# Low key parts doubled per head, so that the second score and low-rank products contract 128 rows

## The chip, the core and the metric

The kernel runs on one core of a Trainium2 chip: TensorE multiplies matrices out of SBUF into PSUM, VectorE, ScalarE and GpSimd work element by element, and DMA queues bring data from HBM. The metric is the device time of one execution in microseconds (us), lower is better. Times come from runs on the chip and from one execution recorded by the hardware profiler.

## What is computed

Two blocks of a network on 512 tokens of width 1024, all in float32. The first block has a convolution, an mLSTM and a feed-forward part. The second has two layers: the first mixes tokens by attention in three branches (compressed, selected and windowed keys), the second by a recurrent mixer; both also attend to 256 memory rows, and both end in a feed-forward part. What matters here:

```python
# attention layer, per branch (12 heads of 64, 4 groups of keys)
s_w = jnp.einsum('bqgrd,bkgd->bgrqk', qc, kwc) * scale - slopes * dist_w
p_w = _masked_softmax(s_w, mask_w)
o_w = jnp.einsum('bgrqk,bkgd->bqgrd', p_w, vwc)
...
# memory attention, both layers (4 heads of 64, 256 rows)
s = jnp.einsum('bshd,bmhd->bhsm', q, k) * (HEAD_DIM ** -0.5)
...
# recurrent mixer: low-rank decay and learning rate (64 wide)
w_log = -jax.nn.softplus(-(w0 + jnp.tanh(zw) @ w2)) - 0.5
a = jax.nn.sigmoid(a0 + za @ a2)
```

With 512 tokens every block of keys is among the selected ones, so that the selected branch is causal attention too.

## The kernel before

**Precision.** TensorE multiplies the type fp32r in one pass. To keep float32's precision the kernel splits an operand into a high part (fp32r) and a low part (the rest), and adds up high x high, high x low and low x high. In the dense products (`dense`, `products`) these are three products of 128 rows and 512 columns for each of the eight feature tiles.

**Heads of 64.** A head has only 64 features, and the array contracts 128 rows. `_stack` (line 1496) makes a tile per head of the queries that holds the high part on the head's own 64 partitions and the low part on the other 64. `_stack_k` (line 1510) makes a tile per head of the keys that holds the high part twice, on both halves, and one more tile for both heads with the low parts, each on its head's own 64 partitions. A score is then two products: the head's query tile against the doubled high key, over 128 rows (high x high and low x high), and the high half of the query against the low key, over 64 rows (high x low). The stationary operand is the query tile, 128 queries wide, so each product is preceded by a load of weights. `_stack_k` is called for the selected and the windowed keys of both pairs of groups in the attention and for the memory's keys in each layer, six times in all.

**Who uses it.** `_nsa_unit` (line 1576) is one block of 128 queries of two heads in one branch: per head the two products into a PSUM bank, an operation of VectorE that adds the distances out of PSUM and takes the minimum, and an exponential on ScalarE; then the division, transposes and the products with the values, 64 wide. A unit has 128, 256, 384 or 512 keys; there are 48 units, so 96 pairs of products. `_mem_att` (line 1376) does the same for the memory with 256 keys: 16 pairs in each layer. `_rw_prep` (line 1793) has two low-rank products for each of six pairs of heads, 512 columns wide: the weights' high part (stationary) against the stacked `zwa` over 128 rows, and the weights' low part against the high half of `zwa` over 64 rows. The low-rank weights come from DRAM with their 64 rows twice, so that `_rw_lora` splits a tile that is already doubled. The gate's low-rank product in `_rw_pair` (line 2094) has three parts of 128 rows and one of 96.

**Order of issue.** The order is written by the program beforehand. Units, memory attention and pairs of heads are generators; `_Side` steps them beside the dense products. `_Clock` estimates when each engine will be done with what was issued; its cost of an fp32r product depends on the columns alone, but the columns that it counts towards TensorE's activity are weighted with the part of the array that the stationary operand fills. `tick` lets steps run beside a dense product only while that activity is high (`hot`), and `keep_warm` issues products of zeros into an unread bank when it is low. All tiles come from 74 slots (`_Slots`) in a ring; a generator starts only if as many slots are free as its `need` says, and `_rw_pair` waits for 12. PSUM has eight banks, taken in the same way. VectorE also writes the low part of every dense weight tile (`wl`), ScalarE the high part (`wh`), both three tiles ahead.

In the profile every instruction carries line 359, that of the recording helper; tiles out of slots are called s, PSUM banks b, the mixer's stacked tiles k.

Of the kernel before, what the change touches and what calls it, by code (L numbers as in the profile page):

```python
# [237 lines left out]
def _region(x):  # L238
    """The partitions and columns of a piece of a tile on chip, or None."""
    if getattr(x.tensor, "_space", None) is None or "DRAM" in str(x.tensor._space):  # L240
        return None
    (w, n), rest = x.ap[0], x.ap[1:]
    p, f = divmod(x.offset, w) if w else (0, 0)
    return p, p + n, f, f + 1 + sum(abs(a) * (b - 1) for a, b in rest)


class _Clock:
    """When each engine comes to the end of what has been issued to it, as far as that is known beforehand: the order of
    issue follows from it."""
# [10 lines left out]
    def hot(self, least):  # L260
        """Whether the tensor engine's last window had so many columns: its clock halves when it idles."""
        while self.win and self.win[0][0] < self.t["tensor"] - WINDOW:
            self.cols -= self.win.popleft()[1]
        return self.cols >= least
# [82 lines left out]
class _Timed:  # L347
    """An engine, or the core, with every issue noted by the clock."""
# [43 lines left out]
def _run(g):  # L392
    """A generator's value, run to its end."""
    while True:
        try:
            next(g)
        except StopIteration as e:
            return e.value


class _Side:
    """Generators whose steps run beside the dense products: of the first few, those whose operands should be done by now."""
# [4 lines left out]
    def add(self, g, need=0, prio=0):  # L407
        """need: the slots that the generator will take, free before it starts; prio: the first of those ready."""
        B = self.B
        self.q.append([max(B.pe, B.clock.step) + B.lat, g, need, False, prio])  # L410
# [4 lines left out]
    def step(self, wait=True):  # L415
        """One step of the generator that is ready first; without wait, only if one is."""
        if not self.q:
            return False
        B = self.B
        n = self.free()  # L420
        e = min([e for e in self.q[:self.width] if e[3] or e[2] <= n] or self.q[:1],
                key=lambda e: (max(e[0], B.pe), -e[4], e[0]))
        if e[0] > B.pe:
            if not wait:
                return False
            B.keep_warm(e[0])
        step, B.clock.step = B.clock.step, 0.0
        e[3] = True
        t = B.sl.taken
        try:  # L430
            next(e[1])
            e[0] = max(B.pe, B.clock.step) + B.lat if B.clock.step else max(B.pe, e[0]) + POLL
            e[2] = max(0, e[2] - B.sl.taken + t)
        except StopIteration:
            self.q.remove(e)
        B.clock.step = max(step, B.clock.step)
        return True
# [6 lines left out]
class _B:  # L444
# [69 lines left out]
    def warm(self, on=True):  # L514
        """Whether zeros keep the tensor engine's clock up."""
        if on:
            z = self.sl.get()
            self.nc.gpsimd.memset(z, 0.0)
            self.zero, self.zps = self.sl.get(F32R), self.ps.get()
            self.acopy(self.zero, z)  # L520
            self.sl.put(z)
        else:
            self.sl.put(self.zero)
            self.ps.put(self.zps)
            self.zps = None

    def keep_warm(self, until):
        """Products of zeros into a bank that nobody reads."""
        while self.zps is not None and (self.pe + 300 < until or not (until or self.clock.hot(HOTF))):
            self.nc.tensor.matmul(self.zps, self.zero[:, 0:128], self.zero, start=True, stop=True)  # L530
# [57 lines left out]
    def hl_g(self, src, scale=None):  # L588
        """The high and the low part of src, or of src times a column: a generator."""
# [15 lines left out]
    def park(self, j):  # L605
        """x's tile to DRAM; its slot is free again."""
        self.nc.gpsimd.dma_start(self.xd[:, j, :], self.x[j])
        self.sl.put(self.x[j])
# [11 lines left out]
    def col_sums(self, accs, nb):  # L620
        """Sums over the partitions, per token: [128 tokens, nb] of each."""
        ps = self.ps.get()
        for i, acc in enumerate(accs):
            for b in range(nb):
                o = 2 * (nb * i + b)
                self.mm(ps[:, o:o + 2], acc[:, 128 * b:128 * b + 128], self.ones[:, 0:2])
        return ps

    def spread(self, cols, nb):
        """Columns [128 tokens, nb] -> the tokens' values on all partitions, in PSUM."""  # L630
# [8 lines left out]
    def rstd_g(self, acc, nb=4, in_psum=False):  # L639
        """Per token (mean of the squares + eps)^-0.5, on all partitions: a generator."""  # L640
# [17 lines left out]
    def rstd2(self, a1, a2):  # L658
        """r1 = rstd of a1's squares; r2 = r1 times the rstd of a2's squares scaled by r1."""
# [128 lines left out]
def _ada_dot(B, e, ts, cb):  # L788
    """One feature tile of the modulation: the rows of its weights times silu(c)."""
# [7 lines left out]
def _ada_side(B, cols, last=False):  # L797
    """Feature tiles of the modulation: a generator."""
# [10 lines left out]
def _mem_prep(B, out):  # L809
    """The memory's rows, split, times both layers' norm weights; their factors: a generator."""  # L810
# [54 lines left out]
def _start(B):  # L865
    """Block 1's h by feature tiles, as the modulation's weights come, and the first projections beside it, all of them open."""
# [46 lines left out]
    h = []  # L913
# [37 lines left out]
def _conv_ops(B, pairs, done):  # L951
    """The 31 taps of two channel tiles, their chains taken in turn, in PSUM."""
# [28 lines left out]
def _gates(B, ps):  # L981
    """Input and forget gates -> rows of the running maximum, columns of g and of exp(-m): a generator."""
# [32 lines left out]
def _mlstm(B, h, q, k, va):  # L1015
    """One head's stabilised memory read, normalised and scaled: a generator of steps."""
# [69 lines left out]
def _conv_ln(B):  # L1086
    """Layer norm over the channels and silu: a generator; leaves B.a."""
# [25 lines left out]
def _qk_conv(B, z, y, c, h):  # L1113
    """The causal convolution of four taps, the last already in y, and silu: a generator."""
# [216 lines left out]
def _ffn(B, h, u, d, sq, gcol, post, mid=None):  # L1331
    """x += g * (silu(h Wg) * (h Wu)) Wd; with sq, h still wants the tokens' factors, from the squares' sums sq."""
# [43 lines left out]
def _mem_att(B, i, t, q, cross):  # L1376
    """Attention of a q tile (two heads, scaled by -1/8) to the memory: a generator."""
# [8 lines left out]
    for hf in range(2):  # L1386
        r0, r1 = 64 * hf, 64 * hf + 64
        sm = B.mp.tile([128, 8], F32, tag="ms", name="ms", bufs=4)
        pr = []
        for bp in range(2):  # L1390
            ps = B.ps.get()
            for b in range(2):
# [3 lines left out]
                B.mm(o, q[hf][r0:r1, qb:qb + 128], B.memS[i][2][r0:r1, m], False, True)  # L1396
# [42 lines left out]
def _compress(B, st):  # L1439
    """Keys and values of the compressed blocks: a generator."""  # L1440
# [55 lines left out]
def _stack(B, z, out=None):  # L1496
    """Two heads' tile, split: per head [high; low], the high parts on the head's own partitions. A generator."""
# [12 lines left out]
def _stack_k(B, z, st, key):  # L1510
    """Two heads' keys, split: per head [high; high], and the low parts. A generator."""
# [6 lines left out]
    low = B.sl.get(F32R)  # L1518
    for hf, t in enumerate(out):
        a, b = slice(64 * hf, 64 * hf + 64), slice(64 - 64 * hf, 128 - 64 * hf)  # L1520
        B.tt(low[a], z[a], t[a].bitcast(F32), OP.subtract)
        B.vcopy(t[b], t[a])
    B.sl.put(z)
    st[key] = out + [low]


def _nsa_comp(B, i, q, st, P):
    """The compressed blocks' branch of two heads, which begins their sum: a generator."""
# [47 lines left out]
def _nsa_unit(B, i, br, b, st, P, mix):  # L1576
    """One block of queries of two heads in the selected or the windowed branch: a generator."""
# [11 lines left out]
    for hf in range(2):  # L1589
        r = 64 * hf  # L1590
# [3 lines left out]
        B.mm(ps[:, :n], q[r:r + 64], k[2][r:r + 64, 0:n], False, True)  # L1594
# [39 lines left out]
def _tok_major(B, src, st, key):  # L1634
    """A tile's transpose: a generator."""
# [26 lines left out]
def _nsa(B, xg, factors):  # L1662
# [8 lines left out]
    for n in NSA_ORDER:  # L1671
# [22 lines left out]
        else:  # L1694
# [5 lines left out]
            elif nm in ("ks", "kw"):  # L1700
                B.side.add(_stack_k(B, t, st, (nm, e)), 3)
# [14 lines left out]
def _wo(B, name, parts, g2):  # L1716
    """x += rhs Wo, in parts as the mixers' shares come; x * g2 in parts, the squares' sums."""
# [62 lines left out]
def _rw_lora(B, p, g):  # L1780
    """One pair's share of the low-rank weights, split: the high and the low parts, side by side. A generator."""
# [11 lines left out]
def _rw_prep(B, p, rkv, R):  # L1793
    """One pair of heads: decays, keys and their products, with the exponents taken about each chunk's middle: a generator."""
# [10 lines left out]
    B.mm(ps, lo[0:64, 256:384], R["zwa"][0][0:64], False, True)  # L1805
# [4 lines left out]
    B.mm(ps, lo[64:128, 384:512], R["zwa"][1][64:128], False, True)  # L1810
# [79 lines left out]
def _rw_blocks(t):  # L1890
    """The diagonal 16 x 16 blocks of [64, 64] matrices that lie 4160 apart: [block, row, column]."""
# [3 lines left out]
def _rw_rows(t):  # L1895
    """The same matrices: [row, matrix, column]."""
# [3 lines left out]
def _rw_inv(B, p, lt, R):  # L1900
    """The inverses of the diagonal 16 x 16 blocks of one pair's triangular matrices, by substitution: a generator."""
# [34 lines left out]
def _rw_half(B, out, ps, mask):  # L1936
    """Four blocks of 128 columns from PSUM, the latter half of each masked."""
# [5 lines left out]
def _rw_pair(B, p, rkv, R, mix):  # L1943
    """One pair of heads, from the projections to its share of the mix: a generator.

    A chunk and head gets the factors of [values | state], [tokens | keys, next state | outputs], whatever the state is.
    """
# [290 lines left out]
```

## Time and profile before

| | us |
|---|---|
| median of 3 runs | 2523.57 |
| lowest and highest run | 2523.26, 2525.66 |
| span of the profiled execution | 2516.8 |
| TensorE busy in the span | 2441.9 |
| VectorE busy | 1470.4 |
| ScalarE busy | 921.5 |
| GpSimd busy | 408.4 |

The span runs from the first to the last instruction. A busy share is an average over stages; the first block takes 540 us, the feed-forward parts some 400 each, the attention layer lies at 945 to 1320 us, the recurrent mixer at 1700 to 2060 us with its last products up to 2120. TensorE's busy time includes the way of a product through the array, so that two products in a row overlap in it; the distance between the starts of two weight loads (PEld) tells better what a product costs.

### The profile page before, as it was taken

The page shows a single profiled execution, that of the slowest core. Times are in us where ns is not written, and L with a number is a line of the kernel's source. Part 1 is how long each engine was busy: PE and PEld are TensorE (multiplying, and loading weights), DVE is VectorE, ACT ScalarE, POOL GpSimd, SP SyncE. Part 2 cuts the span into 40 slices and gives each one's busy share as a digit, 9 for nine tenths or more (in the row PEclk, how much of TensorE's full clock was granted, in tenths as well). Part 3 has the DMA queues.
Part 4 walks back from the last instruction along what each step waited for, and adds up shares of the span by engine and source line. Part 5 has one row for each costly group of instructions (what it writes and reads, how often), then busy time and mean ns, then how long its engine had stood idle before and what let it go on. Part 6 is the DMA issues. An engine that isn't in the chain of part 4 may idle for free.

```text
span 2516.8 us, 32883 instructions
## 1 busy us (share of the span) xinstructions
PE 2441.9 (97%) x12817; PEld 1951.5 (78%) x12817; DVE 1470.4 (58%) x2673; ACT 921.5 (37%) x1554; POOL 408.4 (16%) x523
## 2 busy tenths in 40 slices
PE   7999999899999999999999999999999999999997
PEld 5877778788888888766677888887777777888886
DVE  7998884867333345476775434446764646443443
ACT  5264445253322233345443222233443323222221
POOL 4433334200000012000002000021451432000000
PEclk8999999999999999989899999999999999999998
DMA  8221223725333234212113232243432231223222
GB/s 275 85 75 59 76 67 132 286 93 184 99 86 109 93 95 163 67 36 78 55 34 114 86 104 98 85 138 122 144 86 57 80 72 34 92 80 113 93 88 79
DMA packets 124956, 252.58 MB, mean 100 GB/s; under 512 B 48253, under 2 KB 54829, under 8 KB 124801
## 3 DMA queue, kind: packets, MB, share of 16 engines
q1 hardware_dynamic: 76096, 211.64, 26.2%
q0 software_dynamic: 10352, 32.74, 3.8%
q10 hardware_dynamic: 38352, 6.10, 1.4%
q8 instruction: 100, 1.64, 0.3%
q14 instruction: 56, 0.45, 0.1%
HBM read 234.69 MB, written 15.75 MB: 100 GB/s over the span
## 4 chain that ended last, share of the span: by engine, by line
PE 62%; issue 20%; DVE 12%; POOL 3%; ACT 2%; DMA 1%; POOLq 0%; SPq 0%; DVEq 0%; ACTq 0%
PE b L359 62%; DVE s L359 7%; DVE b L359 3%; POOL s L359 2%; ACT s L359 2%; DVE modc L359 1%; DVE wl L359 1%; ACT wh L359 0%; POOL gt L359 0%; DMA s<-in_w_ada_dram 0%; DMA s<-in_xT_dram 0%; DMA s<-in_w_in_dram 0%; DMA s<-ltd 0%; ACT L359 0%; DMA ident<-in_ident_dram 0%
## 5 line engine op out<-in xcount | busy, mean ns | idle before, releaser
L359 PE MATMUL b<-s,wh 128*128 128x512 f32 (+1 forms) x5456 | 1699.3, 393 | 6.8 <-DVE s L359 6.3
L359 PEld LDWEIGHTS b<-s,wh 128*128 128x128 f32 x5456 | 1018.2, 190 | 226.4 <-issue 10.6
L359 PE MATMUL b<-s,wl 128*128 128x512 f32 (+1 forms) x2728 | 1062.4, 389 | 8.2 <-DVE wl L359 8.2
L359 PEld LDWEIGHTS b<-s,wl 128*128 128x128 f32 x2728 | 516.6, 189 | 115.4 <-DVE wl L359 8.6
L359 DVE TENSOR_TENSOR wl<-wr,wh 128x1024 fp32r<-128x1024 f32 (+2 forms) x313 | 361.0, 1155 | 217.8 <-ACT wh L359 216.3
L359 ACT ACTIVATE wh<-wr 128x1024 fp32r<-128x1024 f32 (+2 forms) x371 | 364.2, 982 | 222.5 <-PE b L359 176.5
L359 DVE TENSOR_TENSOR s<-b,s 128x512 f32<-128x512 f32 (+4 forms) x338 | 200.9, 601 | 394.8 <-PE b L359 359.8
L359 ACT ACTIVATE s<-s 128x512 f32<-128x512 f32 (+5 forms) x315 | 189.0, 610 | 574.2 <-DVE s L359 558.2
L359 PE MATMUL b<-s,s 64*64 64x64 f32 (+13 forms) x2960 | 334.4, 290 | 14.2 <-DVE s L359 10.3
L359 PEld LDWEIGHTS b<-s,s 64*64 64x64 f32 (+3 forms) x2960 | 228.9, 150 | 122.9 <-issue 63.5
L359 DVE TENSOR_TENSOR s<-s,s 128x512 f32<-128x512 f32 (+5 forms) x308 | 196.0, 649 | 130.3 <-ACT s L359 128.3
L359 POOL TENSOR_TENSOR s<-s,s 128x512 f32<-128x512 f32 (+9 forms) x232 | 134.4, 583 | 566.8 <-ACT s L359 524.6
L359 ACT ACTIVATE s<-b 128x256 f32<-128x256 f32 (+5 forms) x257 | 110.7, 460 | 302.6 <-PE b L359 230.3
L359 POOL TENSOR_TENSOR wl<-wr,wh 128x1024 fp32r<-128x1024 f32 x58 | 143.0, 2466 | 254.3 <-ACT wh L359 245.0
L359 DVE SCALAR_TENSOR_TENSOR b<-s,par,b 128x511 f32<-128x511 f32 (+14 forms) x240 | 158.1, 731 | 0.0
L359 DVE SCALAR_TENSOR_TENSOR s<-s,par,s 128x511 f32<-128x511 f32 (+4 forms) x115 | 106.7, 938 | 30.9 <-ACT s L359 29.8
L359 PE MATMUL b<-s 128*128 128x512 f32 (+2 forms) x601 | 103.1, 338 | 0.0
L359 PE MATMUL b<-ident,s 128*128 128x128 f32 (+1 forms) x544 | 80.5, 281 | 13.7 <-DVE s L359 8.9
L359 PEld LDWEIGHTS b<-ident,s 128*128 128x128 f32 (+1 forms) x544 | 63.7, 143 | 32.5 <-DVE s L359 11.8
L359 POOL TENSOR_TENSOR rs_t<-rs_t,mhalf 128x4 f32<-128x4 f32 (+1 forms) x8 | 7.8, 981 | 467.2 <-DVE rs_t L359 467.2
L359 PEld LDWEIGHTS b<-s 128*128 128x128 f32 (+2 forms) x601 | 65.7, 174 | 17.2 <-issue 7.7
L359 ACT ACTIVATE s<-s,par 128x512 f32<-128x512 f32 (+2 forms) x72 | 48.2, 680 | 64.7 <-DVE s L359 64.2
(160 smaller groups left out, 1091.6 us busy)
## 6 DMA issues: line engine op xcount, KB each, us to landing
wr<-in_w_in_dram SPq DMA_DIRECT2D x59, 512.0 KB, 3.3
s<-in_w_ada_dram SPq DMA_DIRECT2D x96, 256.0 KB, 5.9
wr<-in_fu_dram SPq DMA_DIRECT2D x44, 512.0 KB, 3.3
wr<-in_f0u_dram SPq DMA_DIRECT2D x44, 512.0 KB, 3.3
wr<-in_f1u_dram SPq DMA_DIRECT2D x44, 512.0 KB, 3.3
wr<-in_w_rw_dram SPq DMA_DIRECT2D x23, 512.0 KB, 3.6
wr<-in_w_nsa_dram SPq DMA_DIRECT2D x21, 512.0 KB, 3.3
wr<-in_w_o_dram SPq DMA_DIRECT2D x16, 512.0 KB, 3.4
```

The lines of the kernel that those rows point to most:

```text
L359: r = f(*a, **k)
```

## The change

`_stack_k` makes two tiles of low parts instead of one, each with its head's low part on both halves of the partitions: two more copies on VectorE per call. The second product of a score then takes the whole query tile and the head's doubled low tile, over 128 rows; it now also adds low x low. The second low-rank products take all 128 rows of weights and of `zwa`, which were there already. The generators of the keys want 4 slots instead of 3. Docstrings and comments are taken out as well; nothing of them runs.

```diff
@@ _mem_att
-                B.mm(o, q[hf][r0:r1, qb:qb + 128], B.memS[i][2][r0:r1, m], False, True)
+                B.mm(o, q[hf][:, qb:qb + 128], B.memS[i][2 + hf][:, m], False, True)
@@ _stack_k
-    low = B.sl.get(F32R)
-    for hf, t in enumerate(out):
+    low = [B.sl.get(F32R), B.sl.get(F32R)]
+    for hf, (t, l) in enumerate(zip(out, low)):
         a, b = slice(64 * hf, 64 * hf + 64), slice(64 - 64 * hf, 128 - 64 * hf)
-        B.tt(low[a], z[a], t[a].bitcast(F32), OP.subtract)
+        B.tt(l[a], z[a], t[a].bitcast(F32), OP.subtract)
         B.vcopy(t[b], t[a])
+        B.vcopy(l[b], l[a])
     B.sl.put(z)
-    st[key] = out + [low]
+    st[key] = out + low
@@ _nsa_unit
-        B.mm(ps[:, :n], q[r:r + 64], k[2][r:r + 64, 0:n], False, True)
+        B.mm(ps[:, :n], q, k[2 + hf][:, 0:n], False, True)
@@ _nsa
-                B.side.add(_stack_k(B, t, st, (nm, e)), 3)
+                B.side.add(_stack_k(B, t, st, (nm, e)), 4)
@@ _rw_prep
-    B.mm(ps, lo[0:64, 256:384], R["zwa"][0][0:64], False, True)
+    B.mm(ps, lo[:, 256:384], R["zwa"][0], False, True)
...
-    B.mm(ps, lo[64:128, 384:512], R["zwa"][1][64:128], False, True)
+    B.mm(ps, lo[:, 384:512], R["zwa"][1], False, True)
```

## Rows read from the trace of the kernel before

**Rows 1.** The chain that ended last: its shares of the span by engine.

```profile
PE 62%; issue 20%; DVE 12%; POOL 3%; ACT 2%; DMA 1%; POOLq 0%; SPq 0%; DVEq 0%; ACTq 0%
```

**Rows 2.** Stretches: length, busy us (instructions) of PE, PEld, DVE, ACT, POOL, clock, DMA.

```profile
1045.00:1320.00 275.00, 271.03 (x1477) 189.77 (x1476) 197.64 (x571) 132.17 (x332) 12.58 (x21) 0.92 0.15 49
1700.00:2060.00 360.00, 353.72 (x2894) 270.27 (x2894) 216.76 (x505) 135.78 (x294) 133.42 (x292) 0.99 0.34 96
```

**Rows 3.** Who waited for whom, 1045 to 1320: us, times, longest.

```profile
PEld b L359 <- issue: 44.3, 170, 3.3
...
PE b L359 <- DVE s L359: 3.8, 3, 2.9
```

**Rows 4.** Timeline of weight loads, dense: start, length, [idle before].

```profile
1079.77 0.19 PEld L359 LDWEIGHTS b<-s,wl 128*128 128x128 f32 x1
1079.99 0.41 PEld L359 LDWEIGHTS b<-s,wh 128*128 128x128 f32 x2
1080.45 0.19 PEld L359 LDWEIGHTS b<-s,wl 128*128 128x128 f32 x1
```

**Rows 5.** Timeline of weight loads in units of 512 and of 384 keys.

```profile
1086.73 0.19 PEld L359 LDWEIGHTS b<-s,s 128*128 128x128 f32 x1 [0.25 <-issue]
1087.16 0.18 PEld L359 LDWEIGHTS b<-s,s 64*128 64x128 f32 x1 [0.25 <-issue]
1087.59 0.19 PEld L359 LDWEIGHTS b<-s,s 128*128 128x128 f32 x1 [0.24 <-DVE sm L359]
...
1103.33 0.18 PEld L359 LDWEIGHTS b<-s,s 64*128 64x128 f32 x1 [0.19 <-issue]
1103.70 0.19 PEld L359 LDWEIGHTS b<-s,s 128*128 128x128 f32 x1 [0.19 <-issue]
```

**Rows 6.** The same for 256 and then 128 keys, both shapes merged.

```profile
1172.45 1.12 PEld L359 LDWEIGHTS b<-s,s 128*128 128x128 f32 x4 [0.17 <-issue]
1173.70 0.95 PEld L359 LDWEIGHTS b<-s,s 128*128 128x128 f32 x4
```

**Rows 7.** Timeline of weight loads, dense products of 256 columns, three per row pair.

```profile
562.15 0.19 PEld L359 LDWEIGHTS b<-s,wl 128*128 128x128 f32 x1
...
562.51 0.19 PEld L359 LDWEIGHTS b<-s,wl 128*128 128x128 f32 x1
```

**Rows 8.** The gate's product: its 96-row form, and its loads.

```profile
L359 PE MATMUL b<-k,s 96*128 96x512 f32 x6 | 2.4, 399 | 0.0
...
1943.80 0.76 PEld L359 LDWEIGHTS b<-k,s 128*128 128x128 f32 x4
1944.93 1.07 PEld L359 LDWEIGHTS b<-s,s 64*64 64x64 f32 x36 [0.37 <-issue]
```

**Rows 9.** Products of 64 rows by form: 1045 to 1320, then 1700 to 2060.

```profile
L359 PE MATMUL b<-s,s 64*128 64x256 f32 x40 | 16.8, 420 | 0.0
L359 PE MATMUL b<-s,s 64*128 64x512 f32 x24 | 12.0, 499 | 0.0
L359 PE MATMUL b<-s,s 64*128 64x384 f32 x24 | 10.7, 445 | 0.0
L359 PE MATMUL b<-s,s 64*128 64x128 f32 x24 | 9.1, 379 | 0.0
...
L359 PE MATMUL b<-s,s 64*128 64x256 f32 x16 | 6.1, 381 | 0.0
L359 PE MATMUL b<-k,s 64*128 64x512 f32 x12 | 5.9, 495 | 0.0
```

**Rows 10.** Stretches with a burst of units, and one after it.

```profile
1085.80:1094.60 8.80, 8.80 (x22) 4.53 (x20) 5.66 (x19) 6.06 (x17) 0.00 (x0) 0.77 0.18 61
1110.30:1118.20 7.90, 4.78 (x36) 3.57 (x34) 7.66 (x19) 6.88 (x13) 0.00 (x0) 0.98 0.10 19
...
1242.00:1251.00 9.00, 9.00 (x25) 4.65 (x22) 6.09 (x20) 6.17 (x18) 0.00 (x0) 0.81 0.21 68
```

**Rows 11.** VectorE by form: count, busy us, mean ns; the second row is `_stack_k`'s copy.

```profile
L359 DVE CUSTOM_DVE_ANT_0 s<-b,s 128x512 f32<-128x512 f32 x24 | 16.6, 691 | 9.4 <-PE b L359 9.4
L359 DVE CAST s<-s 64x512 fp32r<-64x512 f32 x12 | 5.1, 424 | 0.2
```

More of the change, by code (lines that the diff above doesn't have):

```diff
@@ L1386, in _mem_att @@
     for hf in range(2):
-        r0, r1 = 64 * hf, 64 * hf + 64
         sm = B.mp.tile([128, 8], F32, tag="ms", name="ms", bufs=4)
@@ L1589, in _nsa_unit @@
     for hf in range(2):
-        r = 64 * hf
         ps = B.ps.get()
```

## The prediction

> **What bounds the kernel now.** I read the chain of work that ended last first: TensorE holds 62% of it and another 20% is "issue", time in which an engine waits for nothing that the profile shows [rows 1]. So the next question is where TensorE itself stands without a cause. The table by stretches gives the two places that the change touches: the attention of the second block (1045 to 1320 us) and the recurrent mixer (1700 to 2060 us). In both TensorE is busy nearly throughout (271.0 of 275 us, 353.7 of 360 us), VectorE 72% and 60%, and the granted clock is 0.92 in the first and 0.99 in the second [rows 2]. The waits in the attention say the same: TensorE's sequencer waited for VectorE for 3.8 us, but the weight loads sat idle before "issue" 170 times for 44.3 us [rows 3]. That idle time is what I look at, because nobody releases it.
>
> The order of weight loads shows where it lies. In the dense products three loads follow each other every 0.68 us (1079.77 to 1080.45), 0.227 us for a product of 512 columns, with no idle time noted: the load hides behind the product ahead of it [rows 4]. In a block of queries the loads of a 128-row and a 64-row product take turns, and each step takes 0.43 us at 512 columns and 0.37 us at 384, with 0.19 to 0.25 us of idle before every load [rows 5]. Four loads at 256 columns take 1.25 us from 1172.45 to 1173.70, so 0.313 us each; the four at 128 columns after them take (0.95 - 0.18) / 3, some 0.255 us each [rows 6]. Dense products of 256 columns step at 0.36 / 3 = 0.12 us [rows 7]. The 128-row and the 64-row product wait alike, so it isn't the size of the 64-row product that costs: it is the turn from one shape to the other. The strongest sign is the gate's low-rank product: its fourth part contracts 96 rows after three of 128, and the four loads lie together in 0.76 us without an idle time ahead of them; the next load, of 64 rows, again stood idle for 0.37 us [rows 8]. Ninety-six rows go with 128, 64 rows don't.
>
> **The change part by part.** (1) The second product of each score and of each low-rank pair gets 128 rows. There are 140: in the attention 24 each of 512, 384 and 128 columns and 40 of 256 (24 of the units, 16 of the memory), in the recurrent mixer 12 of 512 and 16 of 256 [rows 9]. The number of columns stays, so a product itself should cost what its dense neighbour costs. Each of them now pays for two turns, one into 64 rows and one out. What one turn costs, from the rows above: at 512 columns 0.43 - 0.227 = 0.203 us; at 384 0.37 - 0.173 = 0.197 us, where 0.173 is an estimate halfway between the dense steps at 256 and 512; at 256 0.313 - 0.12 = 0.193 us; at 128 0.255 - 0.12 = 0.135 us, where 0.12 is taken from the 256 columns as the nearest row and so is rather too much. Two turns for each: attention 24 x 0.406 + 24 x 0.394 + 40 x 0.386 + 24 x 0.27 = 9.7 + 9.5 + 15.4 + 6.5 = 41.1 us; mixer 12 x 0.406 + 16 x 0.386 = 4.9 + 6.2 = 11.1 us; together 52.2 us. The turn out stays where the next product is 64 wide anyway (values after scores): I estimate one in ten, 14 x 0.2 = 2.8 us off, 2 of it in the attention.
>
> (2) What is late next. In the attention the units come in bursts: ten heads' scores one after the other, ten pairs of products. The stretch from 1085.8 to 1094.6 us is one; five of them stand in the trace, that of 1242 is another [rows 10]. By the steps above its 20 products need 8 x 0.227 + 4 x 0.173 + 8 x 0.12 = 3.5 us without turns and 7.2 us with them at full clock. VectorE has 5.7 us of work in it [rows 10], because every head's score is read out of PSUM by an operation of 0.69 us at 512 columns [rows 11], and the eight banks let TensorE run ahead of it by a few heads only. I therefore let such a burst end after 5.5 us (between 3.5, if the banks hold it all, and 7.2, if TensorE waits for each head): 1.7 us saved of 3.7, 2 us given back in each, 10 us in five. In the stretch from 1110.3 to 1118.2 us VectorE is already the one that is waited for: it is busy for 7.7 of 7.9 us and TensorE for 4.8 [rows 10]; what is won shortly ahead of it, one set of six second products or 2 us, is lost there.
>
> (3) Twelve copies more on VectorE (two in each of six calls of `_stack_k`) at 0.424 us, the copy that is there already [rows 11]: 5.1 us, eight of them in the attention. Nearly all have cover, since VectorE has 77 us free there [rows 2]; the four of the second half of the keys can meet the stretch after 1110 us, where there is none. Bounds 0 and 5.1 us, I take 2. The low-rank part needs nothing new, its weights already stand twice in their tile.
>
> (4) The clock. 0.92 over 275 us means that 16% of it, 44 us, ran at 1.2 GHz instead of 2.4; the bursts show it, at 0.77 and 0.81 [rows 2, 10]. Work that would take 22 us took 44. After the change the same columns come in less time, and with full rows. Bounds: nothing, if the waits for VectorE take the place of the turns, and 22 us if all of it goes. The bursts' share is some two thirds, 15 us; I take half of that, 7.5.
>
> (5) The order of issue. The planner counts a product's columns by the part of the array that it fills, so each of the 140 now counts twice as much. That lets side steps start earlier and asks for fewer products of zeros; and the keys hold one slot of 74 more per tile (four, and one for the memory), with 4 free slots wanted instead of 3. No row prices this; it can go either way. In the mixer, where zeros are issued, it is 12 x 256 + 16 x 128 = 5120 columns more, ten products of zeros or 2.3 us at the most [rows 4]; I set it to nothing.
>
> (6) The mixer's 11.1 us: the low-rank products lie among dense work and should give their 4.9; the memory's 6.2 fall where TensorE also runs products of zeros while chains of other engines go on, and I take half. 8 us.
>
> The sum: attention 41.1 - 2 - 10 - 2 - 2 = 25.1; clock 7.5; mixer 8; together 40.6 us. The profiled span is 2516.8 us and the median of the runs 2523.57, so 6.8 us lie around the span; the change doesn't touch them. 2523.57 - 40.6 gives **2483 us**.
>
> One rule speaks against this. The Trainium skill, "TensorE: Matmul & The Clock Gate", section "Part 3: Packing small matmuls — row/col tiling", says that a weight load overlaps products in flight only where its row group is another one. By that rule two 128-row products in a row would not hide the second load, and the sum of (1) would be nothing. The trace disagrees: dense products, all of 128 rows, step at 0.227 us with loads of 0.19 us in between [rows 4].
>
> **The rivals.** A: all of it comes. The banks carry the bursts, the clock stays up and the planner asks for a few zeros less: 52.2 - 2.8 + 15 + 2 = 66 us, 2457 us. For it: VectorE is free for 77 us of the attention. Against it: it isn't free in the bursts.
>
> B: VectorE becomes the bound of the attention. Its 197.6 us and 3.4 of copies would then be 88% of a stretch of 230 us, and its steps come in chains. If the units' second phase waits as the bursts do, half of the attention's 25 us is lost, no clock comes back, and 12.5 + 8 = 20.5 us remain: 2503 us. For it: the stretch at 1110 us [rows 10]. Against it: VectorE waits far more for TensorE than the other way round.
>
> C: nothing comes, since the load of the second product can't hide behind a first one of the same row group. Mechanism here: load, product, load, product at 0.19 + 0.23 us, about the 0.43 of today [rows 4, 5]. Only the copies are left, 2525 us. The dense rows speak against it. It is what the rule of the Trainium skill named above would do.
>
> D, slower: the slots. Five slots fewer and a higher want per step hold the attention's units back until the dense products that cover them are used up. TensorE then stands as between 1110.3 and 1118.2 us, idle for 3.1 of 7.9 us, or 40% [rows 10]. One cycle of a query tile takes some 40 us, so each held cycle costs 16 us; three of the six cost 48, which is more than the gain: 2483 + 48 = 2531 us. It decides from the third cycle on. Against it: the attention isn't short of cover now, TensorE idles for 4 us of 275 [rows 2].
>
> **How the numbers follow.** Forecast 0.60, A 0.17, B 0.14, C 0.03, D 0.06. The forecast's own bounds come from (2), (4) and (5): bursts 7.2 or 3.5 us, clock 0 or 15, so 2468 to 2500. The range takes in A and B: 2455 to 2506 us, and leaves out C, D and the outer edge of the forecast. About 0.2% (5 us) is what a measurement of this kernel can tell from no change. Faster by more than that: forecast, A and B, 0.91. Within: C, 0.03. Slower: D, 0.06.
>
> **What would show it.** Right: the second products in the profile have 128 rows, the waits of weight loads before "issue" fall from 170 times in the attention to a third, pairs at 512 columns outside bursts step at 0.23 us, and the attention's stretch is about 33 us shorter, the mixer 8. In the bursts, idle time of TensorE ended by VectorE takes the place of "issue". The granted clock rises above 0.92. Wrong: pairs at 128 rows that still step at 0.43 us (C); TensorE waiting for VectorE for tens of us (B); loads of the next heads' tables that move by tens of us (D).

## The result, and the profile after

The changed kernel takes 2482.57 us (median of 4 runs, 2478.97 to 2483.98) against 2524.61 of the kernel before in the same comparison; the ratio is 0.9837, interval 0.9824 to 0.9851. The forecast was 2483 with 2455 to 2506. The whole came out as forecast; its parts didn't, and that is what the rest is about.

The two layers can be cut at the sums over the tokens' squares, four small products with a tile of ones that stand at the head of each layer's factors. In the traces they start at 955.9, 1333.1, 1698.0, 2140.7 us before and at 956.0, 1288.5, 1653.8, 2100.9 after. Between the first two lies the attention layer with its output product, between the last two the mixer with its own. The table by stretches of the kernel before for the two layers (length, busy us and instructions of TensorE, weight loads, VectorE, ScalarE, GpSimd, then the granted clock and the DMA):

```profile
956.00:1333.10 377.10, 368.62 (x1918) 268.51 (x1916) 250.27 (x649) 167.98 (x382) 40.01 (x68) 0.94 0.21 70
1698.00:2140.70 442.70, 432.18 (x3585) 330.51 (x3583) 266.00 (x615) 164.81 (x350) 149.35 (x304) 0.99 0.30 84
```

and of the changed kernel:

```profile
956.00:1288.50 332.50, 317.88 (x1918) 250.19 (x1916) 245.69 (x659) 162.18 (x382) 40.30 (x68) 0.98 0.24 80
1653.80:2100.90 447.10, 435.26 (x3629) 335.10 (x3627) 265.64 (x617) 162.33 (x350) 145.36 (x304) 1.00 0.29 84
```

The attention is 44.7 us shorter with the same number of products. The mixer is 4.4 us **longer**, with 45 products more, all of them of zeros (44 between the rounded edges of the rows). The span falls by 39.6 us, 2516.8 to 2477.2; the stretches outside the two layers differ by 0.4 us or less each.

The second products have 128 rows now, so that both products of a score stand in one row, twice the count of [rows 9] (products by form in the attention), and the copies of `_stack_k` have doubled (VectorE, whole trace; compare [rows 11]):

```profile
L359 PE MATMUL b<-s,s 128*128 128x256 f32 x80 | 14.1, 297 | 3.5 <-DVE s L359 3.5
L359 PE MATMUL b<-s,s 128*128 128x512 f32 x48 | 12.9, 406 | 0.0
L359 PE MATMUL b<-s,s 128*128 128x384 f32 x48 | 11.6, 357 | 3.5 <-DVE s L359 3.2 <-ACT s L359 0.4
L359 PE MATMUL b<-s,s 128*128 128x128 f32 x48 | 8.9, 291 | 0.5
...
L359 DVE CAST s<-s 64x512 fp32r<-64x512 f32 x24 | 9.3, 427 | 0.4
```

The waits of the attention after (who waited for whom, us, times, longest; 1045 to 1275 us), which answer to [rows 3]:

```profile
PEld b L359 <- issue: 23.1, 75, 3.1
PEld b L359 <- DVE s L359: 9.2, 10, 1.9
PE b L359 <- DVE s L359: 8.6, 7, 2.7
```

Of 170 waits without a releaser 75 are left, where a third was forecast, and 44.3 us became 23.1; TensorE's wait for VectorE has grown from 3.8 to 8.6 us. A burst of ten heads shows the gain at its purest. This is one in the timeline of weight loads, with its stretch behind it; compare the loads of [rows 5] and the stretch 1085.8 to 1094.6 of [rows 10]:

```profile
1079.34 3.09 PEld L359 LDWEIGHTS b<-s,s 128*128 128x128 f32 x16 [0.81 <-issue]
1082.70 0.30 PEld L359 LDWEIGHTS b<-s,s 128*128 128x128 f32 x2 [0.27 <-DVE sm L359]
1083.17 0.30 PEld L359 LDWEIGHTS b<-s,s 128*128 128x128 f32 x2 [0.18 <-DVE sm L359]
1083.39 0.30 PEld L359 LDWEIGHTS b<-s,wh 128*128 128x128 f32 x2
...
1078.40:1084.00 5.60, 5.50 (x28) 3.91 (x28) 5.12 (x16) 3.29 (x10) 0.00 (x0) 1.00 0.25 94
```

Sixteen loads in a row without an idle time ahead of any, then two short waits for VectorE: 20 products in 4.05 us (1079.34 to 1083.39) where the same burst took 8.7, and at full clock. The other four bursts took 4.05 to 4.31 us, where they took 7.3 to 8.4 before. VectorE is busy for 5.1 of 5.6 us.

What is late next is seen behind the bursts. In the timeline of all engines from 1218.5 us TensorE has loaded one head's scores and then stands idle for 1.9 us, while VectorE works off a weight tile's low part, a reciprocal, a small product, two scalings and two copies out of PSUM, of which the first ends the wait:

```profile
1218.10 1.22 DVE L359 TENSOR_TENSOR wl<-wr,wh 128x1024 fp32r<-128x1024 f32 x1
1218.55 0.30 PEld L359 LDWEIGHTS b<-s,s 128*128 128x128 f32 x2 [0.17 <-issue]
...
1219.62 0.48 DVE L359 TENSOR_SCALAR s<-s,sm 128x128 f32<-128x128 f32 x2
1220.02 1.15 DVE L359 COPY s<-b 128x512 f32<-128x512 f32 x2
1220.76 0.30 PEld L359 LDWEIGHTS b<-s,s 128*128 128x128 f32 x2 [1.91 <-DVE s L359]
```

### The profile page after: what moved, and what is told of

The parts are those of the page before. It is cut to its first block, busy times and chain, and to the rows that moved or that the text cites. A ratio compares the mean times of both kernels' runs of the same rounds, so it can differ in the third digit from the quotient of the medians.

```text
span 2477.2 us, 32995 instructions
## 1 busy us (share of the span) xinstructions
PE 2393.6 (97%) x12862; PEld 1937.2 (78%) x12862; DVE 1465.2 (59%) x2685; ACT 913.0 (37%) x1554; POOL 404.9 (16%) x523
## 4 chain that ended last, share of the span: by engine, by line
PE 62%; issue 17%; DVE 15%; ACT 2%; POOL 2%; DMA 1%; ACTq 0%; POOLq 0%; SPq 0%; DVEq 0%
PE b L359 62%; DVE s L359 9%; DVE b L359 3%; ACT s L359 2%; POOL s L359 1%; DVE wl L359 1%; DVE modc L359 1%; ACT wh L359 0%; POOL gt L359 0%; DMA s<-in_w_ada_dram 0%; DMA s<-ltd 0%; DVE st L359 0%; DMA s<-in_xT_dram 0%; DVE sm L359 0%; ACT L359 0%
## 5 line engine op out<-in xcount | busy, mean ns | idle before, releaser
L359 PE MATMUL b<-s,s 64*64 64x64 f32 (+9 forms) x2960 | 291.4, 280 | 18.8 <-DVE s L359 13.2
L359 PEld LDWEIGHTS b<-s,s 64*64 64x64 f32 (+3 forms) x2960 | 216.2, 149 | 99.0 <-issue 43.3
L359 POOL TENSOR_TENSOR s<-s,s 128x512 f32<-128x512 f32 (+9 forms) x232 | 128.5, 557 | 546.1 <-ACT s L359 499.2
L359 PE MATMUL b<-s 128*128 128x512 f32 (+2 forms) x646 | 118.4, 342 | 0.0
L359 PEld LDWEIGHTS b<-ident,s 128*128 128x128 f32 (+1 forms) x544 | 63.4, 142 | 35.0 <-DVE s L359 14.2
L359 PEld LDWEIGHTS b<-s 128*128 128x128 f32 (+2 forms) x646 | 71.7, 173 | 18.5 <-issue 5.3
```

The source lines that it names most:

```text
L359: r = f(*a, **k)
```

## The experiments

The change does two things at once: it gives the second products 128 rows, and it changes the order of issue, since the planner counts their columns anew and the keys take more slots. The runs take these apart. Theory T is that of the prediction: a turn between a 128-row and a 64-row product costs TensorE some 0.2 us. Theory O is its rival: the other order of issue makes the time.

All of them at a glance: time with its ratio to the kernel before (interval), length of the two layers, time at 1.2 GHz in each of them, and products of zeros in the mixer. Each ratio is to the kernel before as it was measured beside that run (medians from 2521.2 to 2524.6 us). The lengths and the times at 1.2 GHz come from one profiled execution of each kernel: the part ahead of the attention, which the change doesn't touch, took from 955.4 to 960.0 us in the twelve of them, so a difference of two or three us in one column shows little by itself.

| run | us | ratio | attention | mixer | at 1.2 GHz | zeros |
|---|---|---|---|---|---|---|
| before | 2524.61 | 1 | 377.2 | 442.7 | 48.0, 10.2 | 211 |
| changed | 2482.57 | 0.9837 (0.9824 to 0.9851) | 332.5 | 447.1 | 10.2, 3.4 | 256 |
| e1 order after, 64 rows | 2535.31 | 1.0051 (1.0035 to 1.0068) | 380.6 | 456.2 | 54.7, 6.8 | 256 |
| e2 old count, 128 rows | 2468.54 | 0.9786 (0.9772 to 0.9801) | 331.5 | 436.9 | 6.8, 3.4 | 234 |
| e3 old count, 64 rows | 2526.74 | 1.0020 (1.0010 to 1.0029) | 381.9 | 445.5 | 58.5, 6.8 | 234 |
| e4 attention only | 2485.37 | 0.9852 (0.9837 to 0.9866) | 332.4 | 453.5 | 10.2, 6.8 | 256 |
| e5 order before, 128 rows | 2465.36 | 0.9772 (0.9754 to 0.9789) | 328.4 | 436.3 | 3.4, 13.7 | 211 |
| e6 96 rows | 2481.84 | 0.9839 (0.9820 to 0.9859) | 334.2 | 448.9 | 13.8, 6.8 | 256 |
| e7 two and two | 2498.72 | 0.9903 (0.9886 to 0.9920) | 343.4 | 454.9 | 14.1, 6.8 | 265 |
| e8 mixer only | 2522.86 | 1.0006 (0.9996 to 1.0015) | 378.7 | 443.7 | 51.4, 3.4 | 260 |
| e9 every sixth zero out | 2475.61 | 0.9808 (0.9791 to 0.9824) | 332.2 | 440.8 | 10.2, 6.8 | 214 |
| e10 e5 without zeros | 2451.17 | 0.9711 (0.9697 to 0.9726) | 329.6 | 420.3 | 6.8, 47.8 | 0 |

### e1: the order of the changed kernel, 64 rows

The planner is told of the 128-row product, and the 64-row one is issued:

```diff
+    def mm2(self, out, lhsT, rhs, notedT, noted, start, stop):
+        self.nc.tensor._real.matmul(out, lhsT, rhs, start=start, stop=stop)
+        self.clock.note("tensor", "matmul", (out, notedT, noted), {"start": start, "stop": stop})
...
-        B.mm(ps[:, :n], q, k[2 + hf][:, 0:n], False, True)
+        r = 64 * hf
+        B.mm2(ps[:, :n], q[r:r + 64], k[2 + hf][r:r + 64, 0:n], q, k[2 + hf][:, 0:n], False, True)
```

and so in the memory's and the low-rank products.

> The changed kernel with its order of issue, its tiles and its copies kept instruction by instruction, but the 140 second products contract 64 rows again. Theory T (each turn between 128 and 64 rows costs TensorE some 0.2 us, and the clock falls in the bursts that the turns stretch): the gain is gone, 2523 to 2535 us; from the first weights of the attention to the sums behind it about 44 us longer than in the changed kernel; granted clock from 1045 to 1320 us back near 0.92; pairs at 512 columns step at 0.43 us. Theory O (the gain comes from the other order of issue and the row count does nothing): it stays at 2480 to 2487 us. Rule of the Trainium skill, TensorE: Matmul & The Clock Gate, Part 3, that loads overlap only across row groups: it would stay at 2483 too, as the shapes would step alike.

Measured 2535.3 us: with the order of the changed kernel and 64 rows nothing of the gain is left, and the kernel is 0.5% slower than before. The pairs turn again (timeline of weight loads; L476 is the line of `mm2`), and the clock of the attention is back at 0.93 (table by stretches):

```profile
1086.30 0.19 PEld L359 LDWEIGHTS b<-s,s 128*128 128x128 f32 x1 [0.25 <-issue]
1086.73 0.18 PEld L476 LDWEIGHTS b<-s,s 64*128 64x128 f32 x1 [0.25 <-issue]
1087.15 0.19 PEld L359 LDWEIGHTS b<-s,s 128*128 128x128 f32 x1 [0.24 <-DVE sm L359]
...
955.40:1336.00 380.60, 371.63 (x1918) 270.07 (x1916) 253.48 (x659) 168.72 (x382) 40.29 (x68) 0.93 0.21 70
```

So the row count alone is worth 2535.3 - 2482.6 = 52.7 us at this order, 48.1 in the attention and 9.1 in the mixer; the two profiled executions differ by 56.1 us in their spans. Theory O is out, and so is rival C of the prediction.

Since both traces hold the same 12862 weight loads in the same order, the step from each load to the next can be set against its like. In the attention (956 to 1289 us of the changed kernel) the steps differ by 48.5 us in sum:

| kind of step | steps | us |
|---|---|---|
| turn gone, both at 2.4 GHz | 172 | 33.9 |
| turn gone, at 1.2 GHz with 64 rows | 40 | 10.4 |
| no turn, at 1.2 GHz with 64 rows, at 2.4 with 128 | 95 | 14.2 |
| no turn, the other way round | 22 | -2.6 |
| over 0.15 us longer with 128 rows, both at 2.4 GHz (turn or none) | 10 | -6.9 |
| all others | | -0.5 |

A turn at full clock is 33.9 / 172 = 0.197 us on the mean. In the mixer 47 turns are gone, for 9.9 us.

### e2 and e3: the old count of columns, with 128 and with 64 rows

e3 is the changed kernel with 64-row products, noted as such; e2 issues 128-row products in that same order, noted as 64 (eight products of zeros changed places with a neighbour). Slots, wanted slots and copies are those of the changed kernel in both.

```diff
 e2:
-        B.mm(ps[:, :n], q, k[2 + hf][:, 0:n], False, True)
+        r = 64 * hf
+        B.mm2(ps[:, :n], q, k[2 + hf][:, 0:n], q[r:r + 64], k[2 + hf][r:r + 64, 0:n], False, True)
 e3:
-        B.mm(ps[:, :n], q, k[2 + hf][:, 0:n], False, True)
+        r = 64 * hf
+        B.mm(ps[:, :n], q[r:r + 64], k[2 + hf][r:r + 64, 0:n], False, True)
```

> The changed kernel, 128 rows, but the planner notes the second products as 64 rows, as it did before; only the slots and the copies still shape the order of issue. Theory T: the attention is as short as in the changed kernel, within 3 us. For the mixer, which became 4.4 us longer with the change instead of 8 shorter: if the doubled count of columns did it by another order of issue (45 products of zeros more), the mixer is 5 to 12 us shorter than in the changed kernel and the whole 2471 to 2478 us; if the slots or the real pace of the engines did it, the whole stays at 2480 to 2487 us.

> The order of issue of the run with 128 rows and the old count, but 64 rows: against the kernel before, only five slots, the wanted slots and twelve copies differ. Theory T with slots of no weight: 2522 to 2530 us. The slots as a cost of their own (rival D of the prediction): over 2530 us. Against the run with 128 rows and the old count the difference is the row count alone: theory T 41 to 60 us, theory O 0.

2468.5 and 2526.7 us: the row count gives 58.2 us at this order too, 50.4 in the attention and 8.6 in the mixer. The slots and copies alone (e3 against before) cost 0.2%, 4.7 us in the attention and 2.8 in the mixer; that attention had 10.5 us more at 1.2 GHz (58.5 against 48.0), which alone is an estimated 5 us. Rival D isn't there at a size that matters. The doubled count of columns costs 14 us in itself (2482.6 against 2468.5), 10.2 of them in the mixer: 447.1 against 436.9 with 128 rows, 456.2 against 445.5 with 64.

### e4 and e8: one layer alone

e4 leaves the low-rank products and the memory of the second layer as they were; e8 changes nothing but these.

```diff
 e4:
-    B.mm(ps, lo[:, 256:384], R["zwa"][0], False, True)
+    B.mm(ps, lo[0:64, 256:384], R["zwa"][0][0:64], False, True)
 ...
 e8:
-        B.mm(ps[:, :n], q, k[2 + hf][:, 0:n], False, True)
+        r = 64 * hf
+        B.mm(ps[:, :n], q[r:r + 64], k[2][r:r + 64, 0:n], False, True)
```

> Doubled low tiles and 128 rows in the attention layer alone, its memory products included; the mixer's low-rank products and its memory products as before. If the change costs in the mixer: 2476 to 2480 us, the mixer from its first factor sums to those behind it near 442.7 us as before. If the mixer's turns are won and something of the attention's end pushes it: slower than the changed kernel, 2487 to 2494 us.

> 128 rows and the doubled low tile in the mixer alone (low-rank products, memory of the second layer); the attention as before at 377 us. If the mixer's own count of columns and its one slot more bring the other order of issue that costs some 13 us there: mixer 444 to 449 us, the whole 2524 to 2531 us. If the order only moves because the attention ahead of it ended otherwise: mixer about 434 us, the whole 2512 to 2517 us.

e4 takes 2485.4 us, between the two ranges and 1.6 us below the one by which the mixer's turns are won and something else costs: the attention is as short as with the whole change, but its mixer takes 453.5 us instead of the 442.7 of before, though none of its operations is changed. e8 takes 2522.9 us, on neither side of what was expected: its mixer of 443.7 us has the 128 rows, which are worth 9, and still isn't shorter than before. Both have 256 to 260 products of zeros. So the mixer's order of issue moves whether the attention ahead of it changes or the mixer itself, and it costs some 10 us either way. It isn't the count of columns in the mixer alone.

### e5: the order of the kernel before, 128 rows

All engines issue in the order of the kernel before; the tiles for the second copies are taken from the other end of the free slots and not counted as taken, and the copies aren't noted.

```diff
+    x = B.sl.take(F32R)
     for hf, t in enumerate(out):
+        l = x if hf else low
...
+        v.tensor_copy(l[b], l[a])
...
-        return len(self.B.sl.free) - MAIN - sum(e[2] for e in self.q if e[3])
+        return len(self.B.sl.free) + self.B.sl.hidden - MAIN - sum(e[2] for e in self.q if e[3])
```

> 128 rows in all 140 second products, but every engine's order of issue is that of the kernel before; only the twelve copies come in between on VectorE, and the five tiles that they fill lie in slots that the planner doesn't count as taken. Theory T (row count alone, which gave 48 to 50 us in the attention and 9 in the mixer at two other orders): attention about 328 us instead of 377, mixer about 434 instead of 443, the whole 2460 to 2469 us, below the changed kernel. If the order of before hides less of it, because its steps were timed with the turns in them: 2470 to 2483 us.

2465.4 us, as theory T expected and 17 less than the changed kernel. The table by stretches:

```profile
956.00:1284.40 328.40, 314.69 (x1917) 247.98 (x1915) 245.55 (x659) 161.79 (x382) 40.28 (x68) 0.99 0.24 81
1649.40:2085.70 436.30, 423.87 (x3585) 329.86 (x3583) 266.35 (x617) 163.79 (x350) 150.63 (x304) 0.98 0.29 86
```

The attention is shorter by 48.8 us, as at the other orders; the mixer by 6.4. Together these are 55.2 us, the cleanest single number for the change without its side effects; the ratio of 0.9772 is 58 us of 2525.

### e6: 96 rows

```diff
-        B.mm(ps[:, :n], q, k[2 + hf][:, 0:n], False, True)
+        r1, wt = (128, 1.0) if hf else (96, 4.0 / 3)
+        B.mm2(wt, ps[:, :n], q[0:r1], k[2 + hf][0:r1, 0:n], False, True)
```

(here `mm2` only makes the planner count as for 128 rows). Of the pairs, the first head's second product gets the 96 rows; of the low-rank products, the decay's.

> The changed kernel, same order of issue, but the second products of each first head and of the decay contract 96 of their 128 rows (a part of the low x low terms is left out). Theory T (a turn is between 64 and 128 rows, 96 count as 128): as the changed kernel, 2479 to 2487 us. If any product of fewer than 128 rows makes a turn: 70 of the 140 turn again, 2505 to 2512 us.

2481.8 us, the changed kernel's time. The forms show the 96 rows, and the burst still loads sixteen times without an idle time (timeline of weight loads):

```profile
L361 PE MATMUL b<-s,s 96*128 96x512 f32 x12 | 4.7, 395 | 0.0
...
1079.59 3.09 PEld L361 LDWEIGHTS b<-s,s 128*128 128x128 f32 x16 [0.81 <-issue]
```

Set load against load as in e1, the steps on either side of a 96-row product differ by 0.0 us in sum from those with 128. It isn't "fewer than 128 rows" that turns.

### e7: two first products, then two second ones, with 64 rows

```diff
+    qs, pss = [P["q"][hf][:, 128 * b:128 * b + 128] for hf in range(2)], [B.ps.get(), B.ps.get()]
     for hf in range(2):
-        r = 64 * hf
-        ps = B.ps.get()
-        q = P["q"][hf][:, 128 * b:128 * b + 128]
-        B.mm(ps[:, :n], q, k[hf][:, 0:n], True, False)
-        B.mm(ps[:, :n], q[r:r + 64], k[2][r:r + 64, 0:n], False, True)
+        B.mm(pss[hf][:, :n], qs[hf], k[hf][:, 0:n], True, False)
+    for hf in range(2):
+        r, ps = 64 * hf, pss[hf]
+        B.mm(ps[:, :n], qs[hf][r:r + 64], k[2][r:r + 64, 0:n], False, True)
+    for hf in range(2):
+        ps = pss[hf]
```

> The kernel before, 64 rows, but a unit issues both heads' first products and then both second ones, so that a unit has two turns (into 64 rows and out) instead of four; memory and mixer unchanged. Theory T: 96 turns less at 0.14 to 0.2 us, 18 us, and some of the clock, less what another order of issue costs: 2494 to 2510 us; clock of the attention above 0.92. If each 64-row product costs by itself, or a change of the half of the rows is a turn as well: 2518 to 2530 us.

2498.7 us, within what theory T expected, with 64 rows throughout. A cost of each 64-row product by itself is not ruled out by this time alone, since two of them run together here; it is by [rows 8], where 36 loads of 64 rows follow each other and only the first stood idle. But the attention alone gained 33.8 us, more than the turns that went, while the mixer, with another order again, lost 12.2. The loads of a burst say why (512 columns first, 384 last):

```profile
1046.91 0.30 PEld L359 LDWEIGHTS b<-s,s 128*128 128x128 f32 x2 [0.81 <-issue]
1047.58 0.18 PEld L359 LDWEIGHTS b<-s,s 64*128 64x128 f32 x2 [0.37 <-issue]
1048.01 0.30 PEld L359 LDWEIGHTS b<-s,s 128*128 128x128 f32 x2 [0.25 <-issue]
...
1049.65 0.19 PEld L359 LDWEIGHTS b<-s,s 64*128 64x128 f32 x2 [0.25 <-issue]
```

Two 64-row loads together take 0.18 us, as long as one. The second head's product, on the other half of the rows, starts 3 ns after the first's (median of the 48 units), so the two run side by side and not one after the other: 1.10 us for two heads' scores of 512 columns against 1.72 before and, by the steps of [rows 4], 0.91 with 128 rows. The time at 1.2 GHz falls from 48.0 to 14.1 us here as well.

### e9 and e10: the products of zeros

e9 is the changed kernel, e10 is e5, each with the planner's order kept:

```diff
-            self.nc.tensor.matmul(self.zps, self.zero[:, 0:128], self.zero, start=True, stop=True)
+            self.nz += 1
+            if self.nz % 6:
+                self.nc.tensor._real.matmul(self.zps, self.zero[:, 0:128], self.zero, start=True, stop=True)
+            self.clock.note("tensor", "matmul", (self.zps, self.zero[:, 0:128], self.zero), {"start": True, "stop": True})
```

(In e10 the condition is `self.nz < 7`, which leaves the six products of zeros ahead of the mixer.)

> The changed kernel with the same order of issue, but every sixth product of zeros is only noted by the planner and not issued: 43 fewer, as many as the change brought on top. They fill a bank that nobody reads. If the products of zeros themselves cost the mixer its 10 us (they take TensorE's time on the path): mixer 436 to 440 us, the whole 2471 to 2476 us. If they only fill time in which TensorE would wait, and the steps of the other order come late by themselves: mixer within 2 us of 447, the whole 2480 to 2486 us. If the clock falls without them: over 2486 us.

> The version with 128 rows and the order of issue of the kernel before, with the 211 products of zeros of the mixer noted but not issued (they fill a bank that nobody reads). 211 x 0.227 = 48 us of TensorE's time. If they stood on the path throughout: 2420 to 2440 us. If they fill waits and keep the clock: the granted clock of the mixer falls below 0.95 and the whole is 2465 to 2485 us. Between, 2440 to 2462 us, if a part of them stood in the way of steps that were ready.

e9: 2475.6 us, inside the range by which the zeros themselves cost the time; its mixer of 440.8 us is just above that range. The mixer is 6.3 us shorter for 42 zeros less, which by the steps of [rows 4] took 42 x 0.227 = 9.5 us. Some two thirds of the zeros' time lay on the path, then; for the rest, 3.4 us more ran at 1.2 GHz and the weight loads' waits for VectorE and ScalarE grew from 24.0 to 25.8 us.

e10: 2451.2 us, the best of all, 0.9711 of before, and inside the middle range, a part of the zeros in the way of steps that were ready. The mixer (stretch, then waits):

```profile
1654.60:2074.90 420.30, 375.88 (x3373) 296.86 (x3371) 266.13 (x617) 163.11 (x350) 151.17 (x304) 0.94 0.30 89
...
PEld b L359 <- DVE s L359: 31.3, 27, 3.6
PEld b L359 <- ACT s L359: 22.1, 28, 5.0
```

Without zeros TensorE waits openly for VectorE and ScalarE (in e5 these two rows have 16.6 and 3.5 us), the clock falls to 0.94 and 47.8 us run at 1.2 GHz instead of 13.7, and still the layer is 16 us shorter: zeros that keep the clock up cost more here than the clock.

## Why the prediction was right, and where it was not

**Bound and mechanism: right.** The idle time before "issue" was a turn between shapes. e1, e2 and e3 show it at two orders of issue by the row count alone, e5 at a third, e6 that 96 rows belong with 128, e7 with [rows 8] that it hangs on the turn and not on the 64-row product.

**Step 1, the size of a turn: right.** Forecast 0.203, 0.197, 0.193 and 0.135 us at 512, 384, 256 and 128 columns and 41.1 - 2 = 39.1 us in the attention. Measured, as medians of e1's steps at full clock, 0.199, 0.197, 0.195 and 0.145; the mean is 0.197; 172 of them and 40 more that ran at half clock give 33.9 + 40 x 0.197 = 41.8 us. The rows also say what is lost at a turn: in [rows 5] the step of 0.43 us is a load of 0.18 to 0.19 and 0.25 us of idle, near the 0.227 of a dense product. The load no longer hides behind the product ahead, and a turn costs about one load. Whether TensorE empties itself there or only the load is held back, no run tells apart.

**Step 2, what VectorE takes back: too high.** I let a burst end after 5.5 us and gave back 10 us for five, 2 behind them and 2 for copies. The five bursts took 4.05 to 4.31 us, near the 3.5 that TensorE needs by itself: eight heads' sixteen products ran without a wait, and the PSUM banks carry nearly all of it. VectorE's work doesn't go away, it comes later, as waits of up to 1.9 us behind the bursts. In e1's table the longer steps sum to 6.9 us, where I had given back 12. The step that failed is the claim that the banks hold a few heads only.

**Step 4, the clock: too low.** I took 7.5 us, half of the bursts' 15. From e1's table it is 10.4 - 7.9 for the turns that ran at half clock, 14.2 for the rest, less 2.6: 14.1 us, nearly all of the 15. In the kernel before, the clock fell inside each of the five bursts, and what followed at 1.2 GHz is 31 of the 44 us in 1045 to 1320. In the changed kernel no burst is followed by such a stretch; one of 3.4 us is left among the units, at 1221.7 us, just behind TensorE's wait of 1.9 us that is shown above. e7 shows the same fall of the time at 1.2 GHz with 64 rows; since its products on the two halves run together, it doesn't tell whether the shorter burst or the fuller rows keep the clock.

**Steps 3 and 5, copies and order of issue: mis-sized.** Copies and slots cost 4.7 us in the attention (one execution of e3, and by the clock above all), where I had 2 for the copies and nothing for the slots; ten of the twelve copies lie there, not eight. The step that failed in the mixer is the order of issue, which I set to nothing; it costs 13.5 us at 64 rows (442.7 before, 456.2 in e1): 2.8 with slots and copies alone (445.5 in e3), the rest with the doubled count. I had seen the count and taken it for a gain of up to 2.3 us in zeros; there were 45 zeros **more**. "It can go either way" was said, but no bound was put on it, and the mixer's sign came out wrong by it. e9 puts about 6 us of it on the zeros themselves. What makes the planner ask for more of them isn't settled: e4 and e8 do so by changes in different layers, and of the other orders that were tried with 128 rows only that of e2 (436.9 us) comes near that of the kernel before (436.3 in e5).

**Step 6, the mixer's turns: right as far as the rows go,** 8 us forecast, 9.1 and 8.6 measured (6.4 in e5).

**The sum.** Forecast 32.6 us in the attention and 8 in the mixer; it is 44.7 and -4.4. The two misses, 12 us each, cancel, so that 40.6 met 42 by luck; the row count alone would have been 53 to 58. One more thing came out even: I set the 6.8 us between the profiled span and the median apart as time around the span. In the changed kernel the profiled execution took 2478.97 us with a span of 2477.2, only 1.8 us around it, so most of the 6.8 was that the profiled execution of the kernel before was faster than the median. It came out even because that of the changed kernel was, too, by 3.6 us. And by its own terms the forecast's lower bound was 2465.5 us (10 and 7.5 below 2483), not 2468.

**The rivals.** A (all of it, 2457) named what the change does without its side effects: e5 at 2465 is nearer to it than to the forecast. B is seen only in its beginnings, 8.6 us of waits for VectorE. C and D didn't come.

## What to carry to other kernels

Read the distance between weight loads, not the length of products: idle time with no releaser between two shapes can be a turn, and filling a half-empty product with what is already there, or with a doubled tile, takes it away at no cost in columns. When a schedule is worked out by a program, hold its order fixed and change the hardware side alone, then the other way round; otherwise a gain of 55 us and a loss of some 15 are read as one number. And fillers that keep a clock up have a price that is worth measuring by leaving them out.

## What the runs showed of the hardware

A 64-row product between products of 128 rows costs two turns of 0.197 us each (the mean over all columns; 0.145 at 128 columns, 0.195 to 0.199 above, e1 against the changed kernel), about the 0.19 us of one weight load; 96 rows cost none (e6: 0.0 us). Two 64-row products on the two halves of the rows start 3 ns apart and run together (e7). The Trainium skill, "TensorEngine Tiling (Array Packing)", section "Key Properties", says that changing the tiling mode, not just the tile, drains TensorE; the trace agrees as far as the time goes, with 0.197 us for the change and 3 ns for another tile of the same mode. The rule that I had weighed against the change, from the Trainium skill, "TensorE: Matmul & The Clock Gate", section "Part 3: Packing small matmuls — row/col tiling", that loads overlap only across row groups, isn't borne out: sixteen loads of the same 128 rows follow each other without an idle time.

And the clock: leaving out all 211 products of zeros in the mixer brought 34 us more at 1.2 GHz, yet 16 us less time (e10 against e5).
